# A two-layer hybrid encoder on one core: gates rebuilt from logarithm and exponential, a term across halves as biased exponentials, one burst per head's output, and the last sums moved one chunk later

## The chip, the cores and the metric

The kernel runs on one core of one Trainium2 chip. The metric is the device time of one execution in microseconds (us), lower is better. A core has five engines with instruction queues of their own: TensorE (PE in the profile), VectorE (DVE), ScalarE (ACT), GpSimd (POOL) and SyncE (SP), the last of which only issues transfers here. The engines meet at semaphores: an instruction that reads what another engine writes stands at the head of its queue until that is done, and all that is queued behind it stands too.

## What is computed

The reference takes 256 tokens of width 2048 with 16 learned meta tokens in front (272 columns) through two layers. In fp32:

```
proj = h @ w_in         # [GLA q | k | v | output gate r | low-rank decay | NA q | k | v]
o    = o_fwd + o_bwd    # gated linear attention (GLA), 4 heads, both directions
o    = o * rsqrt(mean(o*o) + eps) * norm_w * silu(r)
y    = concat(o, neighbourhood_attention(NA q, k, v, bias)) @ w_out
h    = layernorm(alpha*h + y)
h    = layernorm(alpha*h + relu(h @ w_ff1)**2 @ w_ff2)
```

`silu(r) = r / (1 + exp(-r))` is the gate that this change rebuilds. In the GLA part a key s acts on a query t through the product of the decays between them; with running sums b of log decays this is `exp(b_t - b_s)`, one direction at a time. The meta tokens are dropped from the output.

## The kernel before

**Layout and the main products.** Activations are held with features on the 128 partitions and tokens in the free dimension, 272 columns wide in layer 0 and 256 in most of layer 1. Each weight tile (128 x 1024, fp32) comes by one transfer from SyncE into `raw`; ACT casts it to a high half `wh` (L164), DVE subtracts to get a low half `wl` (L165), and TensorE multiplies three times: `wh` by the activations' high and low halves and `wl` by the high one (L177 to L179 at 272 columns; L173 and L174 at 256, where one matmul of 512 columns takes both halves of the activations). `weights()` makes tiles two ahead of their use, with three buffers each for `raw`, `wh` and `wl`. `by_m` (L207) goes through four output chunks with 16 k-steps each and evicts each chunk; in layer 1 an eviction starts by joining two parts of the accumulator (ACT L186, DVE L187).

**The work beside them.** After each eight k-steps `pump` lets generators go on by some steps: `fg` one step per call, `bg` by a credit of 1.3 per call in the stage of the output gate (the r stage) and 1.1 in the stage of the neighbourhood attention (the NA stage). A step's instructions enter the program there, and are tied behind the latest `wl` in DVE's order; the scheduler of the framework then sets the order on each engine. The order is fixed at build time, so a step that comes one pump earlier changes the queues of all engines behind it.

**The gates.** `ev_r` evicts a chunk of r: ACT `exp(-r)` (L438), POOL adds 1 (L439), ACT copies r (L441), and a foreground generator `silu` (L444) follows: at its second step a DVE reciprocal of one half of the columns, at its third that of the other half (both L448), at its fourth the product r * s (L451).

**A GLA head** (`gla_head`, L462) goes in the background, four heads per layer. The scores of 256 tokens are built in nine levels in the order 7, 0, 1 to 6, 8. For a level, `operands` subtracts running sums on POOL (four instructions, L487), takes the exponential on ACT (L492) and multiplies by q and k on DVE (L493) into a tile `lev` (three buffers); then TensorE forms scores (L517) and ACT (L522) or DVE (L524, by a mask) puts them into A. `across` makes the same for the term between the two halves of the sequence, with four subtractions against one column each on POOL (L500 to L503), one exponential over 544 columns on ACT (L504) and two products on DVE (L505, L506), read by the matmuls L532. The scores of the 16 meta tokens go to `am`, split in high and low parts by `stack` (L231, L232). Then come, for each half e of the head's 256 output columns, two fp32 matmuls by V (L550, L551; each runs as two passes) and one with `am` (L552), a square on ACT (L553), and the end of a step.

**The end.** In layer 1 the last two output chunks, 14 and 15, go through `first` (L936; matmuls L942, L944, L947) for half of the tokens and `second` for the rest, with weights split by ACT L157 and DVE L158. `ln_sums` splits the sums over chunks 0 to 13 into `sp` (through `split`, L225 and L226); `ln_products` multiplies them by ones (four matmuls, L841), called at k-step 18 of chunk 14's `first`. At k-step 18 of chunk 15's `first`, `stats` adds chunk 14 (L972, L973).

Of the kernel before, what the change touches and what calls it, by code (L numbers as in the profile page):

```python
# [52 lines left out]
class Trunk:  # L53
# [194 lines left out]
    def layer(self, l):  # L248
# [4 lines left out]
        with ExitStack() as actx:  # L253
# [5 lines left out]
            self.be = [t(f"be{h}", [P, 2, L + 1]) for h in range(GH)]  # L259
            self.V = [t(f"V{i}", [P, GH * GDV]) for i in range(2)]  # L260
# [66 lines left out]
    def gates(self):  # L327
# [30 lines left out]
        for h in range(GH):  # L358
            for d in range(2):
                z = self.bank()[:, :L]  # L360
                nc.tensor.matmul(z, lhsT=up[:, d, h * GDK:h * GDK + GDK], rhs=lr, start=True, stop=True)
                g = e.tile([P, L], F32, name="gt", tag="gt", bufs=2)
                nc.scalar.activation(g, z, AF.Abs)
                nc.scalar.activation(g, g, AF.Exp, scale=-1.0)
                nc.scalar.activation(g, g, AF.Ln, bias=self.one)
                nc.vector.scalar_tensor_tensor(g, z, 0.0, g, ALU.min, ALU.subtract)
                self.sums(self.be[h][:, d, :], g, d)
                yield

    def sums(self, b, g, d):  # L370
# [62 lines left out]
    def ev_r(self, c, ps):  # L433

        nc, n = self.nc, self.n
        self.y[c] = self.pair(self.yp, "y", c)
        s = self.g2.tile([P, L], F32, name="rs", tag="rs")[:, :n]
        nc.scalar.activation(s, ps, AF.Exp, scale=-1.0)  # L438
        nc.gpsimd.tensor_scalar(s, s, 1.0, 1.0, ALU.mult, ALU.add)  # L439
# [4 lines left out]
    def silu(self, c, s, r):  # L444
        yield
        half = self.n // 2
        for p in (slice(0, half), slice(half, self.n)):
            self.nc.vector.reciprocal(s[:, p], s[:, p])  # L448
# [13 lines left out]
    def gla_head(self, h):  # L462
# [33 lines left out]
        def across():  # L496
            t = level()
            bm, e0 = bf[:, L - 1:L], eb[:, 0:1]
            ts = nc.gpsimd.tensor_scalar
            ts(t[:, 1, :T], bf[:, :T], bm, 1.0, ALU.subtract, ALU.mult)  # L500
            ts(t[:, 0, T:L], bf[:, T:L], bm, -1.0, ALU.subtract, ALU.mult)
            ts(t[:, 1, T:L], eb[:, T:L], e0, -1.0, ALU.subtract, ALU.mult)
            ts(t[:, 0, :T], eb[:, :T], e0, 1.0, ALU.subtract, ALU.mult)  # L503
            nc.scalar.activation(t, t, AF.Exp, scale=1 / TAU)  # L504
# [42 lines left out]
        for e in range(2):  # L547
            o = self.bank()[:, :n]
            c = slice(h * GDV + e * P, h * GDV + e * P + P)
            nc.tensor.matmul(o, lhsT=self.V[0][:, c], rhs=af[:, :n], start=True, stop=False)  # L550
            nc.tensor.matmul(o, lhsT=self.V[1][:, c], rhs=af[:, 384:384 + n], start=False, stop=False)  # L551
            nc.tensor.matmul(o, lhsT=self.VS[:, c], rhs=am, start=False, stop=True)  # L552
            nc.scalar.activation(sq[:, e, :n], o, AF.Square)  # L553
            os_.append(o)
            yield
# [367 lines left out]
    def finish(self, u):  # L923
# [221 lines left out]
```

## Time and profile before

| What | us |
|---|---|
| median of 3 runs before | 2369.97 |
| lowest and highest of the 3 | 2369.04, 2369.99 |
| the profiled execution, its own time | 2369.63 |
| span of the profiled execution | 2367.8 |
| mean granted TensorE clock, share of full speed | 0.998 |

The profile is of one execution. Its page gives the busy time of each engine and the chain of work that ended last. The waits list, for each instruction line of an engine, how long the engine sat idle ahead of it and which instruction of which engine released it ("PE bg L517 <- DVE lev L493: 3.3, 4, 1.2" is 3.3 us in 4 waits, the longest 1.2 us). The timeline lists instructions in order: start, duration, engine and line, what is written and read, a count where equal ones follow, and in brackets the idle time ahead of it with its releaser. Groups give count, total busy time and mean nanoseconds of one. The windows give busy times of the engines by stretches of the span. Starts of successive matmuls lie closer than their durations, since they are pipelined: the distance of starts is their cost.

In the profiled execution the attention stages lie at about 117 to 375 us in layer 0 and 1315 to 1575 us in layer 1, the r stages in the first third of these.

### The profile page before, as it was taken

To read this page: it belongs to the slowest core of one execution; us is meant where nothing else is said; L and a number is where in the kernel's file an instruction comes from. 1 tells how busy PE (TensorE), PEld (TensorE's weight loads), DVE (VectorE), ACT (ScalarE), POOL (GpSimd) and SP (SyncE) were. 2 spreads that over 40 slices of the span, in tenths; PEclk is the share of its full clock that TensorE was granted. 3 is DMA by queue.
4 is the path that set the end of the run, shared out by engine and by line. 5 is a ranking of instruction groups with operands and counts; after the bars stand their busy time and mean duration, and the time that the engine had idled before them with its cause. 6 is when DMAs were issued, how large, how long until landed. Compare 5 with 4: busy or idle time off the path is not lost.

```text
span 2367.8 us, 43289 instructions
## 1 busy us (share of the span) xinstructions
PE 2338.5 (99%) x17354; PEld 2227.6 (94%) x17354; DVE 1576.6 (67%) x2490; ACT 1191.8 (50%) x1987; POOL 286.4 (12%) x453
## 2 busy tenths in 40 slices
PE   9999999999999999999999999999999999999997
PEld 9999999999999999999999899998988888888887
DVE  6688787785544455547577787778866555666666
ACT  6555555564433344444456655555754334444444
POOL 1164320020000000000020454300200000000001
PEclk9999999999999999999999999999999999999999
DMA  7544445556555555555556455446666666666664
GB/s 249 170 141 148 141 142 160 177 178 181 179 179 180 181 181 180 178 179 178 179 171 191 144 156 153 145 152 203 184 193 195 195 191 193 194 195 194 191 195 134
DMA packets 120426, 417.49 MB, mean 176 GB/s; under 512 B 13404, under 2 KB 18396, under 8 KB 120224
## 3 DMA queue, kind: packets, MB, share of 16 engines
q1 hardware_dynamic: 120224, 414.72, 56.3%
q8 instruction: 136, 2.23, 0.4%
q14 instruction: 66, 0.54, 0.1%
HBM read 412.57 MB, written 2.10 MB: 175 GB/s over the span
## 4 chain that ended last, share of the span: by engine, by line
PE 90%; DVE 4%; POOL 2%; ACT 2%; issue 1%; DMA 1%; SPq 0%; ACTq 0%; POOLq 0%; DVEq 0%
PE mm L173 21%; PE mm L177 16%; PE mm L178 16%; PE mm L179 16%; PE mm L174 10%; PE mm L203 5%; POOL lev L487 1%; PE bg L517 1%; DVE wl L165 1%; PE bg L660 1%; PE bg L609 1%; ACT wh L164 0%; DVE lev L493 0%; ACT ns L592 0%; DMA raw<-in_wff 0%
## 5 line engine op out<-in xcount | busy, mean ns | idle before, releaser
L165 DVE TENSOR_TENSOR wl<-raw,wh 128x1024 fp32r<-128x1024 f32 (+1 forms) x764 | 936.0, 1226 | 610.2 <-ACT wh L164 602.2
L164 ACT CAST wh<-raw 128x1024 fp32r<-128x1024 f32 (+1 forms) x764 | 795.8, 1042 | 889.1 <-PE mm L178 347.4
L177 PE MATMUL mm<-x,wh 128*128 128x272 f32 (+2 forms) x2176 | 623.1, 286 | 0.0
L178 PE MATMUL mm<-x,wh 128*128 128x272 f32 (+2 forms) x2176 | 617.3, 284 | 0.0
L179 PE MATMUL mm<-x,wl 128*128 128x272 f32 (+2 forms) x2176 | 616.5, 283 | 0.1
L178 PEld LDWEIGHTS mm<-x,wh 128*128 128x128 f32 x2176 | 408.8, 188 | 0.0
L177 PEld LDWEIGHTS mm<-x,wh 128*128 128x128 f32 x2176 | 407.7, 187 | 1.2 <-issue 0.4
L179 PEld LDWEIGHTS mm<-x,wl 128*128 128x128 f32 x2176 | 407.2, 187 | 0.5 <-DVE wl L165 0.3
L173 PE MATMUL mm<-x,wh 128*128 128x512 f32 x1152 | 398.0, 391 | 0.0
L174 PE MATMUL mm<-x,wl 128*128 128x256 f32 x1152 | 318.0, 276 | 0.2 <-DVE wl L165 0.2
L173 PEld LDWEIGHTS mm<-x,wh 128*128 128x128 f32 x1152 | 216.3, 188 | 44.9 <-issue 0.4
L173 PE MATMUL mm<-y,wh 128*128 128x512 f32 x672 | 230.3, 388 | 0.0
L174 PEld LDWEIGHTS mm<-x,wl 128*128 128x128 f32 x1152 | 216.2, 188 | 0.6 <-DVE wl L165 0.6
L177 PE MATMUL mm<-y,wh 128*128 128x272 f32 x704 | 199.2, 283 | 0.0
L178 PE MATMUL mm<-y,wh 128*128 128x272 f32 x704 | 199.2, 283 | 0.0
L179 PE MATMUL mm<-y,wl 128*128 128x272 f32 x704 | 199.0, 283 | 0.0
L174 PE MATMUL mm<-y,wl 128*128 128x256 f32 x672 | 184.7, 276 | 0.7 <-DVE wl L165 0.7
L173 PE MATMUL mm<-u,wh 128*128 128x512 f32 x480 | 164.7, 388 | 0.0
L487 POOL TENSOR_TENSOR lev<-be 128x128 f32<-128x128 f32 (+1 forms) x256 | 150.9, 619 | 113.0 <-PE bg L517 36.6
L173 PEld LDWEIGHTS mm<-y,wh 128*128 128x128 f32 x672 | 126.0, 188 | 26.0 <-ACT wh L164 0.2
L177 PE MATMUL mm<-u,wh 128*128 128x272 f32 x512 | 144.9, 283 | 0.0
L178 PE MATMUL mm<-u,wh 128*128 128x272 f32 x512 | 144.9, 283 | 0.0
(263 smaller groups left out, 3385.9 us busy)
## 6 DMA issues: line engine op xcount, KB each, us to landing
raw<-in_wff SPq DMA_DIRECT2D x512, 512.0 KB, 3.6
raw<-in_win SPq DMA_DIRECT2D x190, 512.0 KB, 3.6
raw<-in_wout SPq DMA_DIRECT2D x64, 512.0 KB, 3.6
nb<-in_nab SPq DMA_DIRECT2D x16, 352.0 KB, 4.0
xraw<-in_xT SPq DMA_DIRECT2D x7, 272.0 KB, 5.2
out<-acc SPq DMA_DIRECT2D x7, 256.0 KB, 2.4
wraw<-in_wup SPq DMA_DIRECT2D x2, 392.0 KB
raw<-in_win SPq DMA_DIRECT2D x4, 128.0 KB, 2.6
```

The lines of the kernel that those rows point to most:

```text
L164: nc.scalar.copy(wh[:, c], raw[:, c])
L165: self.wl = nc.vector.tensor_tensor(wl[:, c], raw[:, c], wh[:, c].bitcast(F32), ALU.subtract).ins
L173: mm(ps, lhsT=wh[:, c:c + P], rhs=x.joined, start=first, stop=False)
L174: mm(ps[:, T:], lhsT=wl[:, c:c + P], rhs=xh[:, :T], start=False, stop=last)
L177: mm(o, lhsT=wh[:, c:c + P], rhs=xh[:, :n], start=first, stop=False)
L178: mm(o, lhsT=wh[:, c:c + P], rhs=xl[:, :n], start=False, stop=False)
L179: mm(o, lhsT=wl[:, c:c + P], rhs=xh[:, :n], start=False, stop=last)
L203: self.nc.tensor.matmul(ps[m][:, :n], lhsT=parts[p][0][:, c:c + P], rhs=acts[j][parts[p][1]][:, :n], start=j + p == 0, stop=j == nk - 1 an ...
L487: tt = lambda o, x, y: nc.gpsimd.tensor_tensor(o, x, y, ALU.subtract)
L517: nc.tensor.matmul(ps[:, b], lhsT=k[:, b], rhs=q[:, r], start=True, stop=True)
L609: nc.tensor.matmul(ps[hh][:, t * NKEY:t * NKEY + NKEY], lhsT=q[hs, NM + t * P:NM + t * P + P], rhs=k[hs, t, :], start=True, stop=True)
L660: nc.tensor.matmul(r[hs], lhsT=(v2 if rest else v1)[:, t, hs], rhs=p2[:, t, :] if rest else p1[:, 2 * t + hh, :], start=rest, stop=not rest)
```

## The change

Four edits.

1. **Gates.** ACT now writes -r instead of r. The two reciprocals go. At the third step of `silu` ACT takes the logarithm of s = 1 + exp(-r) and the exponential of minus that, which gives y, near 1/s; at the fourth DVE makes one Newton step in three instructions, `min(s, 1e30) * y`, `(that - 2) * y` (the two scalar-tensor-tensor instructions, STT below) and the product with -r.
2. **Across.** The four POOL subtractions and the one exponential become four exponentials on ACT, 16, 256, 16 and 256 columns wide, each with a per-partition bias from a new tile `nb` [128, 4]. `nb` is made in the stage ahead (`sums`) by two POOL instructions of one column for each head and direction, 32 in all.
3. **Output of a head.** The four fp32 matmul pairs of both e come first, then both matmuls with `am` and both squares, in one step instead of two. A head takes one background step fewer.
4. **Last sums.** `ln_products` moves from chunk 14's k-step 18 to chunk 15's, ahead of `stats`.

```diff
         r = self.g2.tile([P, L], F32, name="rv", tag="rv")[:, :n]
-        nc.scalar.copy(r, ps)
+        nc.scalar.mul(r, ps, -1.0)
...
     def silu(self, c, s, r):
-        yield
-        half = self.n // 2
-        for p in (slice(0, half), slice(half, self.n)):
-            self.nc.vector.reciprocal(s[:, p], s[:, p])
-            yield
+        yield
+        yield
         gate = self.g2.tile([P, L], F32, name=f"gate{c}", tag=f"gate{c}", bufs=1)[:, :self.n]
-        self.nc.vector.tensor_tensor(gate, r, s, ALU.mult)
+        nc.scalar.activation(gate, s, AF.Ln)
+        nc.scalar.activation(gate, gate, AF.Exp, scale=-1.0)
+        yield
+        stt(s, s, 1e30, gate, ALU.min, ALU.mult)
+        stt(s, s, 2.0, gate, ALU.subtract, ALU.mult)
+        nc.vector.tensor_tensor(gate, r, s, ALU.mult)
...
     def sums(self, b, g, d, nb):
...
         scan(b[:, d:T], g[:, :T - d], total)
+        for i, sign in ((2 * d, 1), (2 * d + 1, -1)):
+            self.nc.gpsimd.tensor_scalar(nb[:, i:i + 1], total, sign / TAU, 0.0, ALU.mult, ALU.add)
...
         def across():
             t = level()
-            bm, e0 = bf[:, L - 1:L], eb[:, 0:1]
-            ts = nc.gpsimd.tensor_scalar
-            ts(t[:, 1, :T], bf[:, :T], bm, 1.0, ALU.subtract, ALU.mult)
-            ts(t[:, 0, T:L], bf[:, T:L], bm, -1.0, ALU.subtract, ALU.mult)
-            ts(t[:, 1, T:L], eb[:, T:L], e0, -1.0, ALU.subtract, ALU.mult)
-            ts(t[:, 0, :T], eb[:, :T], e0, 1.0, ALU.subtract, ALU.mult)
-            nc.scalar.activation(t, t, AF.Exp, scale=1 / TAU)
+            nb = self.nb[h]
+            cols = slice(0, T), slice(T, L)
+            for i, (b, row, at, sign) in enumerate(((bf, 0, 1, -1), (bf, 1, 0, 1), (eb, 1, 1, -1), (eb, 0, 0, 1))):
+                nc.scalar.activation(t[:, row, cols[at]], b[:, cols[at]], AF.Exp, bias=nb[:, i:i + 1], scale=sign / TAU)
...
-        for e in range(2):
+        columns = [slice(h * GDV + e * P, h * GDV + e * P + P) for e in range(2)]
+        for c in columns:
             o = self.bank()[:, :n]
-            c = slice(h * GDV + e * P, h * GDV + e * P + P)
             nc.tensor.matmul(o, lhsT=self.V[0][:, c], rhs=af[:, :n], start=True, stop=False)
             nc.tensor.matmul(o, lhsT=self.V[1][:, c], rhs=af[:, 384:384 + n], start=False, stop=False)
-            nc.tensor.matmul(o, lhsT=self.VS[:, c], rhs=am, start=False, stop=True)
-            nc.scalar.activation(sq[:, e, :n], o, AF.Square)
             os_.append(o)
-            yield
+        for e, c in enumerate(columns):
+            nc.tensor.matmul(os_[e], lhsT=self.VS[:, c], rhs=am, start=False, stop=True)
+            nc.scalar.activation(sq[:, e, :n], os_[e], AF.Square)
+        yield
...
+        def sums():
+            self.ln_products()
+            stats(DC - 2, 0)
...
-            x[c] = first(c, lambda: stats(DC - 2, 0) if c == DC - 1 else self.ln_products())
+            x[c] = first(c, sums if c == DC - 1 else None)
```

How the queues move shows at three places. Line numbers are those of each kernel: L493, L524 and L165 before are L500, L528 and L165 after, L448 is the reciprocal, L456 to L458 are the Newton step.

On DVE, in the first head of layer 1 with the first gate of that layer. Before, from the copy of level 0's scores on:

```order
L524 COPY_PREDICATED A<-mask,bg 128x2x128
L187 TENSOR_TENSOR jn<-jn,mm 128x256
L165 TENSOR_TENSOR wl<-raw,wh 128x1024
L448 RECIPROCAL rs<-rs 128x128
L524 COPY_PREDICATED A<-mask,bg 128x2x128
L448 RECIPROCAL rs<-rs 128x128
L493 TENSOR_TENSOR lev<-lev,qk_14471 128x2x256 x2
L165 TENSOR_TENSOR wl<-raw,wh 128x1024
```

After, from the same copy on:

```order
L528 COPY_PREDICATED A<-mask,bg 128x2x128
L187 TENSOR_TENSOR jn<-jn,mm 128x256
L165 TENSOR_TENSOR wl<-raw,wh 128x1024
L500 TENSOR_TENSOR lev<-lev,qk_14503 128x2x256
L456 SCALAR_TENSOR_TENSOR rs<-rs,gate_15953 128x256
L528 COPY_PREDICATED A<-mask,bg 128x2x128
L457 SCALAR_TENSOR_TENSOR rs<-rs,gate_15953 128x256
L165 TENSOR_TENSOR wl<-raw,wh 128x1024
```

The next level's operand, which stood behind two reciprocals and a copy, now stands directly behind the weight subtraction, and the first instruction of the Newton step, which reads what ACT makes, stands behind it with a weight subtraction further back.

On ACT, in the first head of layer 0 around its `across`. Before:

```order
L438 ACTIVATE rs<-mm 128x272
L441 COPY rv<-mm 128x272
L504 ACTIVATE lev<-lev 128x544
L164 CAST wh<-raw 128x1024
L522 COPY A<-bg 128x2x128
```

After:

```order
L441 ACTIVATE rs<-mm 128x272
L444 ACTIVATE rv<-mm 128x272
L508 ACTIVATE lev<-be_84,nb_88 128x16
L508 ACTIVATE lev<-be_84,nb_88 128x256
L508 ACTIVATE lev<-be_84,nb_88 128x16
L508 ACTIVATE lev<-be_84,nb_88 128x256
L453 ACTIVATE gate_1913<-rs 128x272
L454 ACTIVATE gate_1913<-gate_1913 128x272
L164 CAST wh<-raw 128x1024
L526 COPY A<-bg 128x2x128
```

Five more activations stand ahead of the weight cast L164; those of `across` read only running sums and `nb`, and no longer what POOL makes in the same step.

On TensorE, at the output of the third head of layer 0. Before (the second e follows 30 rows further on, in the next step):

```order
L648 MATMUL bg<-ident,nms_2191 128x128
L550 MATMUL bg<-A,V_88 128x272
L551 MATMUL bg<-A,V_89 128x272
L552 MATMUL bg<-am,VS 128x272
L177 MATMUL mm<-x_272,wh 128x272
```

After:

```order
L636 MATMUL bg<-ident,nr_2219 128x128
L554 MATMUL bg<-A,V_92 128x272
L555 MATMUL bg<-A,V_93 128x272
L554 MATMUL bg<-A,V_92 128x272
L555 MATMUL bg<-A,V_93 128x272
L558 MATMUL bg<-am,VS 128x272 x2
L177 MATMUL mm<-x_105,wh 128x272
```

Four fp32 matmuls now stand ahead of the first one that reads `am`, and the head's place among the steps of the neighbourhood attention has moved.

More of the change, by code (lines that the diff above doesn't have):

```diff
@@ L259, in layer @@
             self.be = [t(f"be{h}", [P, 2, L + 1]) for h in range(GH)]
+            self.nb = [t(f"nb{h}", [P, 4]) for h in range(GH)]
             self.V = [t(f"V{i}", [P, GH * GDV]) for i in range(2)]
@@ L366, in gates, with sums @@
                 nc.vector.scalar_tensor_tensor(g, z, 0.0, g, ALU.min, ALU.subtract)
-                self.sums(self.be[h][:, d, :], g, d)
+                self.sums(self.be[h][:, d, :], g, d, self.nb[h])
                 yield
-    def sums(self, b, g, d):
+    def sums(self, b, g, d, nb):
         def scan(o, i, start):
@@ L440, in ev_r @@
         r = self.g2.tile([P, L], F32, name="rv", tag="rv")[:, :n]
-        nc.scalar.copy(r, ps)
+        nc.scalar.mul(r, ps, -1.0)
         self.fg.append(self.silu(c, s, r))
     def silu(self, c, s, r):
+        nc = self.nc
+        stt = nc.vector.scalar_tensor_tensor
         yield
-        half = self.n // 2
-        for p in (slice(0, half), slice(half, self.n)):
-            self.nc.vector.reciprocal(s[:, p], s[:, p])
-            yield
+        yield
         gate = self.g2.tile([P, L], F32, name=f"gate{c}", tag=f"gate{c}", bufs=1)[:, :self.n]
-        self.nc.vector.tensor_tensor(gate, r, s, ALU.mult)
+        nc.scalar.activation(gate, s, AF.Ln)
[4 more added lines that the diff above has]
+        nc.vector.tensor_tensor(gate, r, s, ALU.mult)
         self.gate[c] = gate
```

## The prediction

> **What bounds the kernel now.** I read the page's busy times first.
>
> ```profile
> PE 2338.5 (99%) x17354; PEld 2227.6 (94%) x17354; DVE 1576.6 (67%) x2490; ACT 1191.8 (50%) x1987; POOL 286.4 (12%) x453
> ```
>
> TensorE is busy for 2338.5 of the span's 2367.8 us. The change takes no matmul away and adds none, so all that it can win lies in the 29.3 us in which TensorE is idle. TensorE's waits say where these are.
>
> ```profile
> PE mm L203 <- ACT wh L164: 4.8, 1, 4.8
> PE bg L517 <- DVE lev L493: 3.3, 4, 1.2
> PE bg L660 <- DVE p L650: 1.2, 3, 0.9
> ...
> PE bg L532 <- DVE lev L506: 1.0, 1, 1.0
> PE bg L552 <- DVE am L232: 0.8, 1, 0.8
> PE mm L174 <- DVE wl L165: 0.8, 2, 0.7
> ...
> PE bg L841 <- ACT sp L225: 0.4, 1, 0.4
> ```
>
> L203 is the first weight of the program, and L660 belongs to the neighbourhood attention; the edits are not about either. What the edits are about is L517, L532, L552, L174 and L841: 3.3 + 1.0 + 0.8 + 0.8 + 0.4 = 6.3 us. TensorE's timeline shows the largest of them.
>
> ```profile
> 139.39 0.67 PE L532 MATMUL bg<-lev 128*128 128x256 f32 x2 [1.03 <-DVE lev L506]
> ...
> 1331.35 0.68 PE L517 MATMUL bg<-lev 128*128 128x128 f32 x4 [1.19 <-DVE lev L493]
> ...
> 1342.55 0.68 PE L517 MATMUL bg<-lev 128*128 128x128 f32 x4 [0.86 <-DVE lev L493]
> ...
> 1379.63 0.68 PE L517 MATMUL bg<-lev 128*128 128x128 f32 x4 [0.99 <-DVE lev L493]
> ```
>
> Three stalls on L517, 1.19 + 0.86 + 0.99 = 3.04 us, stand in the r stage of layer 1, where the credit let two steps of a head follow each other in one pump. The windows of that stage give the busy times of PE, PEld, DVE, ACT and POOL in turn.
>
> ```profile
> 1325.00:1350.00 25.00, 22.95 (x141) 20.20 (x141) 21.43 (x31) 13.85 (x25) 21.41 (x35) 1.00 0.44 129
> 1350.00:1400.00 50.00, 48.85 (x319) 44.30 (x318) 45.40 (x69) 31.76 (x60) 31.05 (x49) 1.00 0.52 157
> ```
>
> DVE is busy for 45.40 of 50 us there, 91%, against 67% over the span: it is the late engine of this stage. ACT has room (64%).
>
> **Gates.** The rows ahead of the three stalls, ACT's for the first and DVE's for each:
>
> ```profile
> 1326.66 0.63 ACT L492 ACTIVATE lev<-lev 128x512 f32<-128x512 f32 x1 [0.16 <-POOL lev L487]
> ```
>
> ```profile
> 1329.55 0.94 DVE L448 RECIPROCAL rs<-rs 128x128 f32<-128x128 f32 x1
> 1330.40 1.61 DVE L493 TENSOR_TENSOR lev<-lev,qk 128x512 f32<-128x512 f32 x2
> ...
> 1340.26 0.94 DVE L448 RECIPROCAL rs<-rs 128x128 f32<-128x128 f32 x1
> ...
> 1341.73 0.68 DVE L493 TENSOR_TENSOR lev<-lev,qk 128x512 f32<-128x512 f32 x1
> ...
> 1377.90 0.94 DVE L448 RECIPROCAL rs<-rs 128x128 f32<-128x128 f32 x1
> 1378.76 1.57 DVE L493 TENSOR_TENSOR lev<-lev,qk 128x512 f32<-128x512 f32 x2
> ```
>
> The exponential of the first was done at 1327.29, three microseconds before L493 took it up at 1330.40. No L493 here waits for its operand; each stands in DVE's queue behind a reciprocal of 0.94 us. Without it each comes 0.94 earlier, which ends the second stall (0.86) and leaves 0.25 and 0.05 of the others: 0.94 + 0.86 + 0.94 = 2.74. The new order puts the operand ahead of the Newton step at the first place; if a step's instruction stands ahead of it at one of the other two, its price comes off once. The prices:
>
> ```profile
> L448 DVE RECIPROCAL rs<-rs 128x136 f32<-128x136 f32 x16 | 15.7, 988 | 1.8 <-POOL rs L439 1.8
> L448 DVE RECIPROCAL rs<-rs 128x128 f32<-128x128 f32 x16 | 15.1, 943 | 0.8 <-POOL rs L439 0.7
> ...
> L460 DVE SCALAR_TENSOR_TENSOR grs<-gtn,grs 128x272 f32<-128x272 f32 x4 | 1.8, 442 | 0.1
> ...
> L364 ACT ACTIVATE gt<-gt 128x272 f32<-128x272 f32 x16 | 6.9, 432 | 0.5
> ...
> L365 ACT ACTIVATE gt<-gt,one 128x272 f32<-128x272 f32 x16 | 8.4, 523 | 0.6
> ...
> L592 ACT ACTIVATE nms<-nms,mst 16x48 f32<-16x48 f32 x16 | 5.1, 319 | 0.0
> ```
>
> DVE gives up 15.7 + 15.1 = 30.8 us of reciprocals and takes on 2 x 16 x 0.442 = 14.1 us, a net of 16.7 over 16 gates, or 1.04 a gate. ACT takes on a logarithm and an exponential, 2 x 0.432 = 0.86 a gate, 13.8 in all. I book -2.7 + 0.3 = **-2.4 us**; the bounds are 0 (the stalls get another cause) and -3.3, all of L517's waits.
>
> **Across.** What POOL and ACT do for it now, over eight heads:
>
> ```profile
> L500 POOL TENSOR_SCALAR lev<-be 128x256 f32<-128x256 f32 x8 | 14.2, 1774 | 3.8 <-PE bg L517 3.7
> ...
> L503 POOL TENSOR_SCALAR lev<-be 128x256 f32<-128x256 f32 x8 | 10.4, 1299 | 0.0
> ...
> L504 ACT ACTIVATE lev<-lev 128x544 f32<-128x544 f32 x8 | 5.3, 658 | 26.9 <-POOL lev L503 26.9
> ```
>
> ACT stands 26.9 / 8 = 3.4 us per head at L504, with weight casts and evictions behind it, while POOL works through at least 24.6 / 8 = 3.1 us of subtractions. Afterwards two wide exponentials with a bias (523 ns each at the most, the price of L365) and two of 16 columns (319 at the most, L592) make 1.68 us in place of 0.66: ACT works 1.0 us longer and no longer stands for 3.4. The operand is ready some 2.4 us earlier, so the stall at L532 (1.03) goes. So does a part of L174's 0.8, where a weight's low half came late behind a cast held up at L504; I count 0.2. Together **-1.2 us**, bounds -1.8 (all of L174's too) and 0. The 32 one-column POOL instructions, at no more than 1.77 us each by L500, lie in a stage with nothing else on POOL that anyone waits for and many steps ahead of their reader; without that cover one of them would be added to the head's first level, a cost below 2 us once.
>
> **Burst.** The third head of layer 0 before the change:
>
> ```profile
> 257.99 0.62 PE L550 MATMUL bg<-A,V 128*128 128x272 f32 x2
> 258.45 0.62 PE L551 MATMUL bg<-A,V 128*128 128x272 f32 x2
> ```
>
> An fp32 matmul takes 258.45 - 257.99 = 0.46 us, so the other e's two put 0.92 us of work between `am`'s request and its reader, more than the 0.8 that L552 waits: **-0.8 us**. The matmuls themselves stay the same in number. One step fewer per head moves all that follows a head one pump earlier, and so also re-draws which steps of the neighbourhood attention meet; its waits of 0.3 to 1.0 (L660) can come or go. I book nothing, plus or minus 1.5, since 1.2 us is what L660 costs in all.
>
> **Last sums.** TensorE's timeline around L841 and at the last weight tile, and the making of that tile on DVE:
>
> ```profile
> 2331.79 0.28 PE L942 MATMUL mm<-u,x 128*128 128x256 f32 x1
> 2331.91 0.28 PE L944 MATMUL mm<-u,wl 128*128 128x256 f32 x1
> 2332.58 1.12 PE L841 MATMUL bg<-sp,onesr 128*128 128x256 f32 x4 [0.39 <-ACT sp L225]
> 2333.53 0.28 PE L942 MATMUL mm<-u,x 128*128 128x256 f32 x1
> ```
>
> ```profile
> 2342.79 0.28 PE L942 MATMUL mm<-u,x 128*128 128x256 f32 x1
> ```
>
> ```profile
> 2339.55 1.29 DVE L158 TENSOR_TENSOR wl<-raw,x 128x512 fp32r<-128x512 f32 x2 [0.88 <-ACT x L157]
> ```
>
> The bracket understates this one: five starts (L944 and four L841) take 2333.53 - 2331.91 = 1.62 us. At the pace of the products ahead, 2331.91 - 2331.79 = 0.12 us a start, it would be 0.60, so 1.0 us is lost, as `sp`'s parts come one after the other. A chunk later `sp` has long been there. Arriving 1.0 earlier, TensorE meets the last weight tile, which DVE ends at 2340.84; the products of that tile start at 2342.79, so it is still in time. **-1.0 us**, bounds 0 (another wait in chunk 15 takes it back) and -1.0.
>
> **What the change adds.** DVE's first Newton instruction waits for ACT's exponential, and behind it in layer 1 stand copies into A and a weight subtraction. L174's 0.8 us in the waits is the only place where TensorE waited for a low half in this stage, so most of such a wait falls into slack. No row shows this wait. Its bounds are 0 and the 0.86 us of both activations at each of eight gates, 6.9; I take 0.4, near the lower end, since the step between leaves ACT a pump of some 1 to 2 us for it.
>
> Sum: -2.4 - 1.2 - 0.8 - 1.0 + 0.4 = **-5.0 us**. On the profiled execution, 2369.63, that is 2364.6; it stood 0.34 below the median of the runs, and so 2365.0 for the median.
>
> **A rule that speaks against it.** POOL's four subtractions of a level take very different times, by what DVE does beside them:
>
> ```profile
> 1328.32 1.54 POOL L487 TENSOR_TENSOR lev<-be 128x128 f32<-128x128 f32 x4
> 1330.24 5.52 POOL L487 TENSOR_TENSOR lev<-be 128x128 f32<-128x128 f32 x8 [0.38 <-PE bg L517]
> ```
>
> Beside the reciprocals four take 1.54 us; beside two L493 and a weight subtraction eight take 5.52, 2.4 more than twice 1.54. So DVE instructions with two operands hold POOL up for most of the 1.61 + 1.42 us that they run, and reciprocals do not. The Newton step's two new instructions have two operands, 0.88 us a gate, 14.1 in all, against more than 24.6 us of POOL's work removed in `across`; POOL's levels in head 0 have no `across` beside the first gates, so there the loss comes first. The Trainium skill says the same (SBUF — State Buffer, "SBUF: two separate sides"): the pair of ports that VectorE shares with GpSimd is an exclusive lock for the whole instruction, taken by VectorE instructions with two SBUF inputs. These rows agree. By the rule alone the levels' exponentials would become late, which is the first rival.
>
> **The rivals.**
>
> *The waits only move.* POOL, held up by 0.88 us a gate, hands its operands over later, ACT's exponential comes later by that and by the gates' 0.86, and L493 waits for it where it waited behind a reciprocal. Then the -2.4 is gone and half of the rest of the r stage (0.6): 2365.0 + 2.4 + 0.6 = 2368.0. For it: POOL is busy for 21.41 of 25 us at 1325. Against: at the first stall the exponential was 3 us early.
>
> *Slower.* In layer 1 DVE stands at the Newton step's first instruction for ACT, with a weight subtraction behind it, and TensorE waits for that low half. It decides if DVE stands past the weights' slack at all eight gates. At 0.86 us, and the (1.8 + 0.8) / 16 = 0.16 by which POOL was already late at a reciprocal, it is 1.0 us each and +8 in all; L517 then gains nothing, and 1.2 + 0.8 + 1.0 = 3.0 stay: 2370.0 - 3.0 + 8 = 2375.0. For it: DVE at 91%, and L174's wait. Against: DVE has a us more per gate, and the activations are issued a step earlier.
>
> *More than forecast.* Less load on DVE and POOL also ends the waits that I left standing, 1.2 (L660), 0.9 (rest of L517) and 0.6 (rest of L174), and the 0.4 for added waits does not come: 2365.0 - 3.1 = 2361.9. For it: DVE and POOL both get lighter. Against: L660 waits for a softmax, which no edit shortens.
>
> *An edit that does nothing.* The burst takes away only one wait, and might do no more than move a neighbour: that is in the 1.5 above.
>
> **How the numbers follow.** About 0.2%, 4.7 us, is what a measurement of this kernel can tell from no change, so faster means under 2365.2. My forecast has 0.60 and reaches from 2362.5 to 2367 by its terms' bounds, with a little over half of it, 0.38, under 2365.2 as the edge lies just above its middle. More gain has 0.14, all faster. Waits that only move have 0.18, within 0.2%. Slower has 0.08. That makes faster 0.52, same 0.40, slower 0.08. The range from 2360.5 to 2369.6 holds the forecast, most of the larger gain and most of the waits that only move; it leaves out the slower case.
>
> **What would show it.** Right: no L517 stall of 0.8 or more between 1325 and 1400, DVE's share there near 80%, ACT no longer standing for POOL at the exponentials of `across`, TensorE not idle at the products of `am`, and the four products of `sp` at the pace of their neighbours. Wrong: L493's successor waiting for ACT's exponential; idle time on DVE at the first Newton instruction with TensorE waiting for `wl` soon after; new waits in the NA stages of more than 1.5 us together, or an idle time at chunk 15's new products.

## The result, and the profile after

The changed kernel takes 2377.49 us (median of 7 runs, 2376.94 to 2378.93) against 2369.99 for the kernel before (7 runs): 1.0033 of it, with a 95% interval from 1.0024 to 1.0043. It is 7.5 us slower, where 5.0 us faster was forecast and the range ended at 2369.6.

The profiled execution took 2378.41 us, with a span of 2376.6. The busy times, and then TensorE's waits:

```profile
PE 2343.2 (99%) x17354; PEld 2231.8 (94%) x17354; DVE 1562.0 (66%) x2490; ACT 1208.1 (51%) x2043; POOL 266.0 (11%) x453
```

```profile
PE bg L792 <- ACT sp L225: 4.6, 2, 2.6
PE bg L521 <- DVE lev L500: 4.0, 5, 1.3
PE bg L665 <- DVE p L655: 2.5, 2, 1.9
...
PE bg L650 <- DVE ns L601: 0.4, 2, 0.3
...
PE bg L536 <- DVE lev L510: 0.2, 1, 0.2
```

With the new line numbers, L521 is what was L517, L536 was L532, L650 was L645 and L665 was L660. As forecast, L532's 1.0 has shrunk to 0.2, and the waits for `am` and for `sp` at the last sums have left the list. The waits at the levels have not shrunk (4.0 against 3.3), those at L665 have doubled, and there is a new line: L792, the two products that average the squares of a head's output, waits 4.6 us in two places. Before, this line (then L787) waited for nothing.

The count of TensorE's instructions is the same, and yet it is busy for 4.7 us longer. The timeline around the first of the two new waits, in the first head of layer 0, shows why:

```profile
150.33 0.28 PE L179 MATMUL mm<-x,wl 128*128 128x272 f32 x1
152.58 1.07 PE L792 MATMUL bg<-sp,onesr 128*128 128x272 f32 x2 [1.97 <-ACT sp L225]
153.45 0.43 PE L177 MATMUL mm<-x,wh 128*128 128x272 f32 x1
153.68 0.43 PE L178 MATMUL mm<-x,wh 128*128 128x272 f32 x1
...
156.17 0.34 PE L177 MATMUL mm<-x,wh 128*128 128x272 f32 x1
...
156.47 0.29 PE L179 MATMUL mm<-x,wl 128*128 128x272 f32 x1
156.60 0.28 PE L177 MATMUL mm<-x,wh 128*128 128x272 f32 x1
```

After the idle 1.97 us the same matmuls of 272 columns start 0.23 us apart, and from 156.5 on 0.13 apart again. The windows of one microsecond have the granted clock in the third column from the end:

```profile
151.00:152.00 1.00, 0.00 (x0) 0.00 (x0) 0.97 (x4) 0.28 (x1) 0.00 (x0) 1.00 1.00 274
152.00:153.00 1.00, 0.39 (x1) 0.19 (x1) 0.87 (x3) 0.89 (x2) 0.00 (x0) 0.94 0.64 258
153.00:154.00 1.00, 0.94 (x4) 0.94 (x5) 0.50 (x2) 0.79 (x2) 0.00 (x0) 0.50 0.18 74
155.00:156.00 1.00, 1.00 (x7) 1.00 (x6) 0.93 (x3) 0.00 (x0) 0.00 (x0) 0.50 0.54 82
157.00:158.00 1.00, 1.00 (x11) 1.00 (x10) 0.77 (x3) 0.22 (x1) 0.00 (x0) 1.00 0.57 229
```

The clock falls to half for some 3.4 us. The same follows the second wait (2.62 us, to 1361 us) and a wait of 1.93 at L665 (to 1432 us): three falls in this execution, none in the kernel before (apart from the last ten microseconds or so of either, after TensorE's last matmul). Twelve matmuls from 153.45 to 156.17 take 2.72 us in place of 1.48, and with L792 and the edges I estimate about 1.6 us a fall.

The products of the main weights come in the same order in both kernels, so the start of the n-th of them in one trace against the other shows where time is lost and won. By that the changed kernel gains 1.3 us at 140 us (L532), loses 4.3 up to 156 (the wait and the fall), is 2.3 behind at the end of layer 0's attention and 0.9 when layer 1's begins, loses 4.5 from 1348 to 1364, 3.2 from 1424 to 1436, is 9.4 behind at the end of layer 1's, gets 1.0 back at the last sums and ends 8.4 behind.

### The profile page after: what moved, and what is told of

Its sections match the earlier page's. It is cut to its first block, busy times and chain, and to the rows that moved or that the text cites. A ratio compares the mean times of both kernels' runs of the same rounds, so it can differ in the third digit from the quotient of the medians.

```text
span 2376.6 us, 43308 instructions
## 1 busy us (share of the span) xinstructions
PE 2343.2 (99%) x17354; PEld 2231.8 (94%) x17354; DVE 1562.0 (66%) x2490; ACT 1208.1 (51%) x2043; POOL 266.0 (11%) x453
## 4 chain that ended last, share of the span: by engine, by line
PE 92%; DVE 2%; POOL 2%; issue 2%; ACT 1%; DMA 0%; SPq 0%; ACTq 0%; POOLq 0%; DVEq 0%
PE mm L173 20%; PE mm L177 17%; PE mm L178 17%; PE mm L179 17%; PE mm L174 10%; PE mm L203 6%; POOL lev L494 2%; PE bg L521 1%; PE bg L665 1%; DVE wl L165 1%; PE bg L614 1%; ACT wh L164 0%; PE bg L350 0%; PE mm L947 0%; PE mm L962 0%
## 5 line engine op out<-in xcount | busy, mean ns | idle before, releaser
L165 DVE TENSOR_TENSOR wl<-raw,wh 128x1024 fp32r<-128x1024 f32 (+1 forms) x764 | 935.3, 1225 | 632.2 <-ACT wh L164 624.6
L164 ACT CAST wh<-raw 128x1024 fp32r<-128x1024 f32 (+1 forms) x764 | 795.8, 1042 | 903.9 <-PE mm L178 338.1
L174 PE MATMUL mm<-x,wl 128*128 128x256 f32 x1152 | 318.3, 276 | 0.0
L174 PEld LDWEIGHTS mm<-x,wl 128*128 128x128 f32 x1152 | 216.8, 188 | 0.0
L174 PE MATMUL mm<-y,wl 128*128 128x256 f32 x672 | 184.7, 275 | 0.7 <-DVE wl L165 0.7
```

The source lines that it names most:

```text
L164: nc.scalar.copy(wh[:, c], raw[:, c])
L165: self.wl = nc.vector.tensor_tensor(wl[:, c], raw[:, c], wh[:, c].bitcast(F32), ALU.subtract).ins
L174: mm(ps[:, T:], lhsT=wl[:, c:c + P], rhs=xh[:, :T], start=False, stop=last)
```

## The experiments

Times are medians; differences are against the kernel before, measured beside each group of kernels on the same chip (2370.38, 2370.36, 2370.53 and 2369.90 us in the four groups, so kernels of different groups compare to about half a microsecond). Ratios have their 95% interval.

**Without the burst.** Edits 1, 2 and 4; the loop over e and its two steps are those of before.

```diff
-        columns = [slice(h * GDV + e * P, h * GDV + e * P + P) for e in range(2)]
-        for c in columns:
+        for e in range(2):
             o = self.bank()[:, :n]
+            c = slice(h * GDV + e * P, h * GDV + e * P + P)
...
+            yield
```

> The change without its third edit: the head's output stays in two steps. Theory S (steps): the loss comes from the step that the burst takes away, by which the products of the mean (L792 in the changed kernel) are reached one pump after the squares and not two, so TensorE stands 2.0 and 2.6 us there and runs at half clock for some 3 us after each. Then here there is no such stall, the granted clock is 0.998 as before, and the time falls by 10 to 12 us against the full change: 2365 to 2368. Theory G (gates): the loss comes from the logarithm that stands in ScalarE's queue for GpSimd with the squares behind it, whatever the steps. Then the mean's products wait here too, 1 to 2 us a layer: 2373 to 2378. Theory B (both are needed): as under S.

Measured: 2368.90 us, -1.5, ratio 0.9993 (0.9985 to 1.0002); no wait at the mean's products, no fall of the clock. That is a microsecond above theory S's range, and theory G is out as it stood: with the step back, the logarithm ahead of the squares does no such harm.

**The burst with the old number of steps.** The full change and one more empty step.

```diff
             nc.scalar.activation(sq[:, e, :n], os_[e], AF.Square)
         yield
+        yield
```

> The full change, with one more empty step behind the burst, so that a head has as many steps as before. Theory S: the step count is the cause and not the order of the matmuls, so no wait of 1 us or more at the mean's products, clock 0.998, 2364 to 2368. Theory G: the logarithm still stands ahead of the squares, waits of 1 to 2 us a layer stay, 2373 to 2378. Theory B: as under S.

Measured: 2367.60 us, -2.8, ratio 0.9988 (0.9979 to 0.9997), no fall of the clock. So it is the step and not the order of the matmuls; one empty `yield` is worth some 10 us here.

**The burst alone.**

> The kernel before with the third edit alone. Theory S: the step is missing here too, so the mean's products stand 1.5 to 2.5 us in each layer, with a fall of the clock where it is near 2: 2373 to 2378. Theory G and theory B: without the logarithm in ScalarE's queue the squares are done some 2 us sooner, the mean's products wait less than 1 us, no fall of the clock: 2368 to 2371.

Measured: 2373.85 us, +3.5, ratio 1.0012 (1.0003 to 1.0021). TensorE's waits:

```profile
PE bg L661 <- DVE p L651: 3.8, 3, 2.2
PE bg L517 <- DVE lev L493: 3.8, 4, 1.5
PE bg L788 <- ACT sp L225: 1.6, 1, 1.6
```

The mean's products wait in layer 1 only, for 1.6, and the attention's products (L661) for 3.8 where it was 1.2. The time lies in theory S's range and above that of G and B, so the step alone costs. But S had a wait in both layers, and layer 0 has none: it takes the gates too to reach the 2.0 and 2.6 of the full change, which is the part of theory B that holds. The eleven runs fall into two groups, five from 2372.05 to 2372.52 and six from 2373.85 to 2374.59, their means 1.8 us apart. The profiled execution (2372.05) is of the lower one, and it shows an idle 2.17 us at L661 with no fall behind it.

**The gates alone.**

> The kernel before with the first edit alone. Theory S and theory B: nothing is lost, the L517 stalls are partly won: 2367 to 2370. Theory G: the squares wait behind the logarithm and the mean's products behind them, and the Newton step keeps VectorE waiting: 2373 to 2378.

Measured: 2373.25 us, +2.9, ratio 1.0014 (1.0005 to 1.0023). No wait at the mean's products, but the levels wait 3.8 (3.3 before), L536, the product of the across term, 1.8 in all where it was 1.0, as GpSimd's four subtractions are still there, and the product with `am` (L556 here) 1.2 where it was 0.8. S and B missed, and G has the time but not the place: the gates cost by themselves, a little at each of these.

**The across term alone.**

> The kernel before with the second edit alone. Theory P (ScalarE stood for GpSimd, and the products of the across term waited for that): the wait of 1.03 at L532 goes and part of the wait for the low half at L174, and GpSimd has more room: 1.2 to 1.6 us less than before. Rival: the 1.0 us that the four exponentials are longer than the one holds up casts and evictions, and what is won at L532 is lost at L517: within 0.5 us of before or above.

Measured: 2367.18 us, -3.2, ratio 0.9987 (0.9979 to 0.9996). It is at least twice what was forecast. In the profile L532 no longer waits, and neither does L552 for `am`, 0.8 before; and the third stall at L517 has fallen from 0.99 to 0.51.

**The full change with the old reciprocals** (edits 2 to 4).

```diff
-        nc.scalar.activation(gate, s, AF.Ln)
-        nc.scalar.activation(gate, gate, AF.Exp, scale=-1.0)
-        yield
-        stt(s, s, 1e30, gate, ALU.min, ALU.mult)
-        stt(s, s, 2.0, gate, ALU.subtract, ALU.mult)
+        for p in (slice(0, half), slice(half, self.n)):
+            self.nc.vector.reciprocal(s[:, p], s[:, p])
+            yield
```

> The full change with the reciprocals of before, so edits two to four. If the costs simply add up (burst alone +3.5, across -1.3, sums -1.0): +1.2 against before, and all gates cost 6 of the 7.5. If the long idle times at the mean's products in the first heads come of the logarithm standing ahead of the squares: the wait there is 0 in layer 0 and 1.0 to 1.6 in layer 1 as with the burst alone, and no clock fall in the r stages. If the missing step alone makes them: 2.0 and 2.6 us and half clock after them as in the full change, +5 or more.

Measured: 2368.08 us, -2.3, ratio 0.9994 (0.9985 to 1.0003). The mean's products wait 0.4 us in all. The costs of the single edits do not add up: the plain sum was +1.2, and a wait of 1.0 to 1.6 was expected in layer 1. With the burst in place the new gates cost 9.4 us, with the steps restored only 2.0 (the next one against the second).

**The same with the extra step.**

> Edits two to four with one more empty step behind the burst and with the reciprocals: what the burst, the across term and the sums are worth when the steps stay where they were. By the waits of before: -1.2 (L532) -0.8 (the wait for am) -1.0 (sums), 3.0 less than before, and 0 to 1 less than the same with the new gates. If the new gates are worth their 2.4 at L517, it is 2 us slower than the full change with the extra step.

Measured: 2365.58 us, -4.8, ratio 0.9982 (0.9973 to 0.9991). This is the fastest of the kernels here that leave nothing out, and it beats both the kernel before and the changed one, by more than the 3.0 that the waits of before gave. With edits 2 and 4 in place there are thus four kernels: 2365.6 with the old steps and the old gates, 2367.6 with the new gates, 2368.1 with one step fewer, 2377.5 with both. The step costs 2.5 by itself and the gates 2.0, together 11.9: the larger part, 7.4, comes only where the two meet. The waits at the levels are 2.9, less than with the new gates (3.6):

```profile
PE bg L517 <- DVE lev L496: 2.9, 4, 1.2
```

**Filling the idle time.** The full change with 16 matmuls of no use just ahead of the mean's products in the first head of each layer.

```diff
         p = self.bank()[:, :src.shape[-1]]
+        for j in range(fill):
+            self.nc.tensor.matmul(p, lhsT=self.ones_r[n], rhs=self.x[j][0][:, :src.shape[-1]], start=True, stop=True)
```

> The full change with 16 more matmuls of 272 or 256 columns, of no use, written to the bank of the mean just ahead of its products in the first head of each layer: they run while TensorE would stand for the squares. Theory C (idle time near 2 us makes the clock fall to half for some 3 us): no fall at 152 and 1361 us, the third at 1432 stays, 1.5 to 1.8 us less for each that goes, in all 2.5 to 3.5 less than the full change although 32 matmuls are added, as 16 take 2.0 us and the waits were 2.0 and 2.6. Rival (the clock falls by load or at set times, not by idle time): the falls stay, no gain, or up to 0.5 more.

Measured: 2373.75 us, ratio to before 1.0016 (1.0007 to 1.0025), 3.7 less than the full change's 2377.49. In layer 0 the 16 take the place of the whole wait, in layer 1 a wait of 0.76 is left; the third wait stays:

```profile
150.75 2.16 PE L792 MATMUL bg<-x,onesr 128*128 128x272 f32 x16
152.87 0.86 PE L794 MATMUL bg<-sp,onesr 128*128 128x272 f32 x2
```

```profile
1359.78 0.84 PE L794 MATMUL bg<-sp,onesr 128*128 128x256 f32 x2 [0.76 <-ACT sp L225]
```

```profile
1429.17 0.44 PE L665 MATMUL bg<-p,nv 128*64 128x128 f32 x4 [1.92 <-DVE p L655]
```

The windows have a clock of 1.00 at 152 and 1361 us and of 0.50 from 1431 on. Adding work where TensorE idled took time off: theory C holds, and the two falls, at 1.6 each, make 3.2 of the 3.7.

**The logarithm of exp(-r) with a bias of one.** ScalarE's queue keeps its order and no longer waits for GpSimd.

```diff
-        nc.gpsimd.tensor_scalar(s, s, 1.0, 1.0, ALU.mult, ALU.add)
+        u = self.g2.tile([P, L], F32, name="ru", tag="ru")[:, :n]
+        nc.gpsimd.tensor_scalar(u, s, 1.0, 1.0, ALU.mult, ALU.add)
...
-        nc.scalar.activation(gate, s, AF.Ln)
+        nc.scalar.activation(gate, s, AF.Ln, bias=self.one)
...
-        stt(s, s, 1e30, gate, ALU.min, ALU.mult)
+        stt(s, u, 1e30, gate, ALU.min, ALU.mult)
```

> The full change, but the logarithm is taken of exp(-r) with a bias of one, and GpSimd's 1 + exp(-r) goes to a tile of its own that only the Newton step reads. ScalarE's queue has the same order; it no longer waits for GpSimd. Theory Q (the squares are late because they stand behind a logarithm that waits for GpSimd, 1.2 us in the first head of layer 0): the idle time at the mean's products falls from 2.0 and 2.6 to 0.5 to 1.3, no clock fall in the r stages, 2370 to 2373. Rival N (the two-operand instructions of the Newton step load VectorE and hold GpSimd up, and that is the delay): within 1.5 us of the full change, 2376 to 2378.

Measured: 2376.14 us, +5.6, ratio 1.0024 (1.0014 to 1.0033). In layer 0 the wait falls from 1.97 to 0.46 and its clock fall goes, 3 us won there. In layer 1 it stays at 2.62 to the hundredth, and a level waits 2.1 where it was 1.3, which gives back over half. By its time this is rival N's range; theory Q holds for layer 0 only.

**Without the Newton step** (the two scalar-tensor-tensor instructions left out).

```diff
-        stt(s, s, 1e30, gate, ALU.min, ALU.mult)
-        stt(s, s, 2.0, gate, ALU.subtract, ALU.mult)
-        nc.vector.tensor_tensor(gate, r, s, ALU.mult)
+        nc.vector.scalar_tensor_tensor(gate, r, -1.0, gate, ALU.mult, ALU.mult)
```

> The full change without the Newton step: the two scalar-tensor-tensor instructions are left out and the gate is -r times minus exp(-log(s)), so its refinement is not computed. The logarithm still waits for GpSimd. Theory Q: the squares are as late as in the full change, about 2 us of idle time at the mean's products and the clock falls stay, 2374 to 2377. Rival N: GpSimd's subtractions come back from some 0.61 to 0.58 us or below, the waits at the levels fall by 1 us or more and those at the mean's products by 0.9, 2370 to 2373.

Measured: 2369.08 us, -1.5, ratio 0.9995 (0.9986 to 1.0003), 8.4 less than the full change. The wait in layer 1 is 0.96, in layer 0 0.27, although the logarithm still waits for GpSimd. It is faster than either theory had it. So rival N is right that the Newton step makes most of the delay, but it held two things, VectorE's time and GpSimd.

**Both mends** (the extra step and the logarithm of exp(-r)).

> Both mends at once: the extra step behind the burst and the logarithm of exp(-r) with a bias of one. With the extra step alone it was 2367.6, with the old reciprocals 2365.6. Theory Q: what the gates still cost with the extra step (2.0) is ScalarE standing for GpSimd, so it ends at 2365 to 2366.5. Rival N: it is the Newton step's hold on GpSimd and VectorE, so 2367 to 2368.

Measured: 2368.54 us, -2.0, ratio 0.9991 (0.9982 to 1.0001): with the step restored the mend of ScalarE's wait gains nothing (-2.8 without it), and both ranges missed.

**The Newton step spread over the steps.** Nothing is left out.

```diff
         yield
-        yield
         gate = self.g2.tile(...)
...
         stt(s, s, 1e30, gate, ALU.min, ALU.mult)
+        yield
         stt(s, s, 2.0, gate, ALU.subtract, ALU.mult)
```

> The full change, but the gate's work is spread over three steps as the reciprocals were: logarithm and exponential at the second step, the first instruction of the Newton step at the third, the second and the product at the fourth. Nothing is left out, and as many two-operand instructions run on VectorE. Theory D (the cost is that 1.3 us of the Newton step and the product stand in one piece on VectorE, ahead of the weight subtraction, the joining of the accumulator and the sum of squares): the idle time at the mean's products in layer 1 falls from 2.6 by 0.4 to 0.9, 2372 to 2375. Theory H (it is GpSimd, held up by two-operand instructions): unchanged, 2376 to 2378.

Measured: 2370.47 us, +0.6, ratio 1.0003 (0.9994 to 1.0011), 7 less than the full change. The wait at the mean's products in layer 1 is 1.41, in layer 0 0.52; the profile has one fall of the clock in place of three, and the levels wait 2.9. That is theory D, by more than it had booked, and theory H is out: as many two-operand instructions run, and the loss is gone. The edit also brings the logarithm and the exponential one step forward, so it does not show that the piece on VectorE made all of it.

**The spread with the extra step, and no Newton step with the extra step.**

> The same spread with the extra empty step behind the burst. With the extra step alone it was 2367.6, with the old reciprocals too 2365.6. Theory D: at most 2366.5. Theory H: 2367 to 2368.5.

> The extra empty step, and the Newton step left out, so the gate's refinement is not computed: the lower end for gates by logarithm and exponential. If all that the gates cost with the extra step (2.0 over the reciprocals) is the Newton step's two instructions, the levels' waits come down below those with reciprocals (2.9), and it ends at 2363 to 2365; if it is ScalarE's two instructions, it stays at 2367 to 2368.

Measured: 2366.37 us, -3.5, ratio 0.9985 (0.9976 to 0.9994), and 2364.98 us, -4.9, ratio 0.9979 (0.9970 to 0.9988). The first meets D's bound; its 0.7 over the extra step alone is hardly more than the 0.6 by which the kernel before differs between the groups. The second is the first of the two readings expected for it: the levels wait 2.3, and what the gates cost with the extra step is gone with the Newton step's two instructions, while ScalarE's two remain. It is only level with the reciprocals (-4.8), so here the logarithm and the exponential win nothing over two reciprocals even at their cheapest.

## Why the prediction was wrong, step by step

**The burst: "-0.8", and for the moved steps "nothing, plus or minus 1.5".** This is the step that failed: with the one step put back the same change is 2.8 us faster (2367.60), inside the range. The wait for `am` went as booked, though the across term alone ends it too. But a head has one step fewer, and what I weighed for that was the neighbourhood attention's waits. I did not follow the next two steps of the same head. Before, the products of both e lay in one pump, the sum of squares and its split in the next, the mean's products in a third. Here is the kernel before, with the last product of `am` and the mean's products in its first head:

```profile
147.98 0.49 PE L552 MATMUL bg<-am,VS 80*128 80x272 f32 x1
...
154.20 0.41 PE L787 MATMUL bg<-sp,onesr 128*128 128x272 f32 x2
```

They lie 6.2 us apart. With one step fewer the burst and the sum of squares fall into one pump and the mean's products into the next, about 3 us on. From burst to mean runs a chain through three engines, and the pump was what hid it. In layer 1 of the changed kernel the chain, ACT first, then DVE, then TensorE, was:

```profile
1356.16 0.41 ACT L453 ACTIVATE gate<-rs 128x256 f32<-128x256 f32 x1
1356.61 0.42 ACT L454 ACTIVATE gate<-gate 128x256 f32<-128x256 f32 x1
1356.93 1.03 ACT L164 CAST wh<-raw 128x1024 fp32r<-128x1024 f32 x1
1357.87 0.36 ACT L186 COPY jn<-mm 128x256 f32<-128x256 f32 x1
1358.13 0.66 ACT L559 ACTIVATE sq<-bg 128x256 f32<-128x256 f32 x2
1360.27 0.42 ACT L441 ACTIVATE rs<-jn 128x256 f32<-128x256 f32 x1 [1.48 <-DVE jn L187]
...
1360.90 0.39 ACT L225 CAST sp<-sq 128x256 fp32r<-128x256 f32 x1
```

```profile
1357.43 0.42 DVE L456 SCALAR_TENSOR_TENSOR rs<-rs,gate 128x256 f32<-128x256 f32 x1
1357.89 0.43 DVE L457 SCALAR_TENSOR_TENSOR rs<-rs,gate 128x256 f32<-128x256 f32 x1
1358.35 0.42 DVE L458 TENSOR_TENSOR gate<-rv,rs 128x256 f32<-128x256 f32 x1
1358.69 1.22 DVE L165 TENSOR_TENSOR wl<-raw,wh 128x1024 fp32r<-128x1024 f32 x1
1359.83 0.41 DVE L187 TENSOR_TENSOR jn<-jn,mm 128x256 f32<-128x256 f32 x1
1360.16 0.42 DVE L561 TENSOR_TENSOR sq<-sq 128x256 f32<-128x256 f32 x1
```

```profile
1355.36 0.59 PE L558 MATMUL bg<-am,VS 80*128 80x256 f32 x2
1361.34 1.04 PE L792 MATMUL bg<-sp,onesr 128*128 128x256 f32 x2 [2.62 <-ACT sp L225]
```

The squares were done at 1358.79. Their sum, on DVE, came at 1360.16, because the whole Newton step, the product, a weight subtraction and the joining of the accumulator stood ahead of it in the queue; and the split on ACT came after an eviction that waited 1.48 us for that same joining. Spreading the Newton step took this wait from 2.62 to 1.41, leaving it out to 0.96. The long wait at the neighbourhood attention (1.93 at L665) comes with the missing step too: every kernel here with one step fewer has one of 1.9 to 2.2 there, none with the step put back.

**The gates: "-2.4 us", bounds 0 and -3.3.** Wrong in sign. Alone they cost 2.9, with the steps restored 2.0, with the burst 9.4. DVE did get lighter, 40.06 of 50 us against 45.40 in the same window (41.67 with the extra step, where TensorE gets through more in that window), but TensorE's waits at the levels stayed (4.0). Of the three stalls the first went, as forecast; the third stayed, at 1.13, with a new one of 1.18 behind it; the second changed its cause:

```profile
1340.73 0.42 ACT L453 ACTIVATE gate<-rs 128x256 f32<-128x256 f32 x1 [0.41 <-POOL rs L442]
1341.06 1.03 ACT L164 CAST wh<-raw 128x1024 fp32r<-128x1024 f32 x1
```

```profile
1342.12 1.22 DVE L165 TENSOR_TENSOR wl<-raw,wh 128x1024 fp32r<-128x1024 f32 x1 [1.32 <-ACT wh L164]
1343.26 0.68 DVE L500 TENSOR_TENSOR lev<-lev,qk 128x512 f32<-128x512 f32 x1
```

```profile
1344.09 0.68 PE L521 MATMUL bg<-lev 128*128 128x128 f32 x4 [1.26 <-DVE lev L500]
```

The level's operand stands behind a weight subtraction that DVE could not start, idle for 1.32 us, since the cast it reads stood behind the logarithm on ACT, which waited for GpSimd and took 0.42 itself. But that is only what came last. The operand's own exponential ended at 1342.92, 0.3 before DVE took it up, after GpSimd's subtractions, which had stood behind GpSimd's 1 + exp(-r):

```profile
1340.11 0.59 POOL L442 TENSOR_SCALAR rs<-rs 128x256 f32<-128x256 f32 x1 [1.06 <-ACT rs L441]
1340.67 1.46 POOL L494 TENSOR_TENSOR lev<-be 128x128 f32<-128x128 f32 x4
```

```profile
1342.31 0.61 ACT L499 ACTIVATE lev<-lev 128x512 f32<-128x512 f32 x1
```

So by these rows only about 0.3 of the 1.26 would go without the late weight subtraction, and with the logarithm freed of GpSimd the stall was 2.09. I had sought the reciprocal ahead of each late operand and not asked what stands there next. The first rival, that the waits only move and the operand's exponential comes late, has this right; its price did not.

**Added waits: "0.4".** I named DVE at the first Newton instruction with a weight subtraction behind it. The instructions that mattered stood behind others of the same step: the squares behind the logarithm on ACT, the joining and the sum of squares behind the Newton step on DVE. In layer 0 no single one of them decides: the wait of 1.97 falls to 0.46 without the logarithm's wait for GpSimd, but also to 0.27 without the Newton step and to 0.52 with it spread. In layer 1 the logarithm's wait makes no difference (2.62 without it); there the Newton step on DVE makes most of it (0.96 without it).

**The second rival, slower at 2375.0,** had the sign and nearly the size, by another road: no weight's low half came later than before (L174 waits 0.7 where it was 0.8).

**The rule on the shared ports** (the Trainium skill, SBUF — State Buffer, "SBUF: two separate sides"). With the extra step GpSimd's subtractions of 128 columns average 614 ns beside the reciprocals, 651 beside the new gates and 624 with the Newton step spread, which is the rule's direction. But in the changed kernel itself they average 609 (620 before), and 605 in the one with the Newton step spread, which is 7 us faster: this was not the main cost.

**Across: "-1.2", bounds -1.8 and 0.** The mechanism held: ACT no longer stands ahead of the exponentials, where it stood 26.9 us in all. The size was off: alone it is worth 3.2, and with the wait at L532 those for `am` and half of a stall at the levels go, 2.3 in all. The burst booked the same 0.8 for `am`; it can be won only once.

**Last sums: "-1.0".** Right. In chunk 15 the four products start without an idle time, and the next line follows 0.47 later, at TensorE's pace; the curve of starts shows 1.0 won:

```profile
2349.12 0.63 PE L846 MATMUL bg<-sp,onesr 128*128 128x256 f32 x4
2349.59 0.38 PE L977 MATMUL bg<-acc,ones 128*128 128x128 f32 x2
```

**What no term had:** three falls of the clock in the profiled execution, about 1.6 us each, 4.8 of the 8.4 that it ends behind. Without them the changed kernel would still have been slower. This execution is one of three at 2378.4 to 2378.9, with a granted clock of 0.995; the other four lie at 2376.9 to 2377.5 with 0.996, so that the median run probably has one fall fewer.

The 2.0 that the gates cost with the steps restored goes with the Newton step's two instructions (-4.9 without them, -4.8 with the reciprocals), and the mend of ScalarE's wait gained nothing there. What stays open is how much of it is VectorE's time and how much is GpSimd held up; no run took GpSimd out alone.

## What to carry to other kernels

Where generators are pumped beside a bound engine, the number of steps between a producer and its consumer is a buffer: before merging two steps, walk the chain of the next two through every engine and compare it with one pump. Count what an edit puts into one queue in one piece, not only its sum, and for each stall that is to go ask what stands in that queue next. A wait of about 2 us on TensorE can cost nearly twice its length, as the one of 1.97 did with the 1.6 of the fall behind it.

## What the runs showed of the hardware

The granted clock fell to 0.50 for some 3.4 us after idle times of TensorE of 1.92 to 2.62 us, at an estimated 1.6 us a fall; while TensorE has work, the profiles show no fall after 1.60 or less. Between these the length alone does not decide: 1.90, 2.09, 2.10 and 2.17 us in four profiles left the clock alone. The longest of these is in the profile of the burst alone, at L661, with the clock at 1.00 before and after:

```profile
1426.91 0.44 PE L661 MATMUL bg<-p,nv 128*64 128x128 f32 x4 [2.17 <-DVE p L651]
```

```profile
1426.00:1428.00 2.00, 1.09 (x17) 0.92 (x17) 2.00 (x6) 1.43 (x3) 0.00 (x0) 1.00 0.24 84
1428.00:1430.00 2.00, 2.00 (x18) 2.00 (x18) 2.00 (x4) 0.37 (x1) 1.27 (x3) 1.00 0.68 229
```

That kernel's runs come in two groups 1.8 us apart, the faster ones at a granted clock of 0.998 (one at 0.997) and the slower ones at 0.997, so the same gap can fall on either side.

The clock records of the traces show what decides. In each profile the clock changes only at whole periods of 3.413 us: the three falls of the changed kernel begin 1208.32 and 71.68 us apart, 354 and 21 periods. Where these periods lie against the program differs from execution to execution. What counts is the idle time within one period. In the sixteen profiles, while TensorE has work, a period with 1.88 us idle or more was followed by one at half clock in all seven cases, one with 1.72 or less never, and of the two between, with 1.82 and 1.84, the first was and the second was not. The 2.17 us above lay across two periods, with 1.72 in the second. Here is the period with 1.82, in the kernel with the Newton step spread, and the one behind it:

```profile
1423.89:1427.31 3.42, 1.59 (x21) 1.42 (x22) 3.32 (x6) 2.73 (x7) 0.49 (x2) 1.00 0.49 151
1427.31:1430.72 3.41, 3.41 (x18) 3.41 (x17) 2.33 (x5) 0.94 (x2) 1.74 (x4) 0.50 0.83 269
```

The Trainium skill (TensorE: Matmul & The Clock Gate, "Part 1: The HAM clock gate") has the clock set by a window of about 3.4 us that runs freely, whatever the kernel does, which fits the length of the falls, the periods and the two groups. Its advice to avoid idle gaps over about 3 us ("Why this matters for your kernels") is too generous here: 1.92 was enough.
